# A decoder layer with 32 routed experts on one core: experts over 64 slots cut in two, scale and shift moved, the first branch hinted, the last norm reordered

## The chip, the core and the metric

The kernel runs on one core of a Trainium2 chip. The metric is the time of one execution in device microseconds (us), the median of several runs. The kernel before takes 1881.35 us (three runs, 1880.34 to 1883.35).

The core has five engines with one instruction stream each: TensorE (PE, matrix products), VectorE (DVE), ScalarE (ACT), GpSimd (POOL) and SyncE (SP). Transfers between the memory outside and the core's own memory go through DMA queues, which the engines feed. PE writes into PSUM, and DVE and ACT read from there.

## What is computed

One decoder layer for 512 tokens of width 1024. Two token mixers (a gated MLP and a dilated attention) give a residual sum, which a LayerNorm closes. Then come a second norm with scale and shift, a router that takes 4 of 32 experts for each token, the experts, and a last norm. Cut to the part that the change concerns:

```
h   = norm(t) * scale + shift                    # (512, 1024); t is the first LayerNorm's output
top_v, top_e = top_k(h @ w_router + b_router, 4)
top_w = softmax(top_v)
for each expert e, for its tokens:
    g = min(h @ w_gate[e] + b_gate[e], 7)
    u = clip(h @ w_up[e] + b_up[e], -7, 7)
    y[tok] += top_w * (((u + 1) * g * sigmoid(1.702 * g)) @ w_down[e] + b_down[e])
out = layer_norm(t * alpha + gate2 * y) * g2 + b2
```

Every expert has three matrices of 1024 x 1024 in f32, 12 MiB together. The reference's inputs are fixed, and so are its counts. Of the 2048 pairs of token and slot, experts 0 to 31 get: 8, 167, 35, 2, 43, 32, 124, 1, 71, 27, 74, 123, 44, 69, 14, 75, 12, 29, 58, 9, 45, 371, 58, 116, 34, 85, 169, 4, 26, 91, 6, 26. The kernel learns them only while it runs.

## The kernel before

**Front part** (to about 640 us). The token mixers run in f32 products made of three passes. For each of four blocks of 128 rows, `norms` makes both norms, and `route` the router's logits, the choice, and one-hot tables (tA, tC at L868, tV), from which PE sums up a slot table: for each expert, which token stands in which of its slots. `route` also scales and shifts h on POOL (L822, L823, two passes over 128 x 1024) and writes it to memory as h2d. From the table come the words `gidx` (rows to gather for each block of 128 slots, `gidx2` for half rows), `wslot` (weights of the slots) and `levw` (three bits for each expert: 0 for at most 64 slots, then one step for each further 64). The same table is waited for by the first gather.

**Expert stage** (from 641 us). The experts run in order, 0 to 31. The weights stream in as 384 units of 1 MiB, 12 for each expert (four of gate, four of up, four of down), into 17 buffers (`NLAND`). `free(u)` on SP starts the load of unit u + 17 once unit u has been used, so the stream runs 17 units ahead of PE at most. Each expert's rows are gathered from h2d by POOL, transposed on PE and copied to xT by ACT (`tr_x`, two copies of 128 x 512), one expert ahead.

What an expert does is chosen by `tc.If(lev > 0)` (L1356), which is a branch on every engine:

- `narrow` (at most 64 slots): the 64 columns of xT use half of PE's columns, so the matmuls run in two column groups, h = 0 and 1, each of which takes its own half of the weight's columns (gate L1088, up L1123, down L1146; biases L1053).
- `wide` (over 64 slots): all 128 columns of xT in full-width matmuls (gate L1091, up L1126, down L1149; biases L1049), and then, for over 128 slots, `further` blocks of 128 slots (L1179) behind a branch of their own (L1191). A further block with at most 64 slots runs like a narrow expert. A wide expert gives its gate's four buffers free only behind `further(e, 0)`, and its up's four behind `further(e, 1)`.

In both, `up` makes the first half of its columns, then the second, and transposes the first half's activations (`tr_act`, L1057) between matmuls of the second; `down` transposes the rest behind its third k tile. `y_out` (L1157) multiplies by the slot's weight and gate2 and adds the rows to ysum in memory by a scatter. `tr_x` for the next expert stands between up and down (`next_rows`). For branches, `mark_branch_hint_location` on PE names the branch that comes next. It stands behind the first bias of `up` for a narrow expert, behind the first k tile of `down` for a wide one; the first branch (expert 0) has none. The order of PE, ACT, DVE and SP in this stage is the order of the text (`manual_schedule`, L1350).

**Last norm** (`Finish`). The rows without the last expert's part are loaded while expert 31 runs; `early` (between gate and up) makes statistics and scaling of row blocks 0 and 1 on DVE, ACT and POOL, `middle` (between up and down) fetches the last expert's rows and treats blocks 2 and 3 on DVE (L1275 statistics, L1283 and L1284 scaling), and `add` treats the last expert's own rows.

Of the kernel before, what the change touches and what calls it, by code (L numbers as in the profile page):

```python
# [35 lines left out]
NLAND = 17  # L36


def host_consts():

    cst = np.zeros((P, 4 * P + NE), np.float32)
# [4 lines left out]
    cst[:, 3 * P + NE:] = np.eye(P)[::-1]  # L46
# [23 lines left out]
def layer(tc, I, out, dump=None, n_exp=NE):  # L70
# [27 lines left out]
    gidx = cp.tile([P, P], I32, name="gidx")  # L98
    wslot = cp.tile([P, P], F32, name="wslot")

    gidx2 = cp.tile([P, P], I32, name="gidx2")
    wslot2 = cp.tile([P, P], F32, name="wslot2")
    levw = cp.tile([1, 4], I32, name="levw")
# [329 lines left out]
    SP.dma_start(flip, I["cst"][:, 3 * P + NE:])  # L433
# [271 lines left out]
    for i in range(2):  # L705
        SP.dma_start(col2[:, i], rowd[1 + i].rearrange("(k p) -> p k", p=P))
    wr = f.tile([P, KT, NE], F32, name="wr")
# [10 lines left out]
    row("sc2", rowd[1:2])  # L718
    row("sh2", rowd[2:3])
# [4 lines left out]
    SP.dma_start(pow8, I["cst"][:, 3 * P:3 * P + NE])  # L724
    iota_e = iota[:, :NE]
# [87 lines left out]
    def route(r):  # L813
# [8 lines left out]
        G.tensor_tensor(h, h, rows["sc2"], op=ALU.mult)  # L822
        G.tensor_tensor(h, h, rows["sh2"], op=ALU.add)  # L823
# [27 lines left out]
        PE.matmul(pcnt, oneb, ohb_, start=r == 0, stop=r == 3)  # L851
# [73 lines left out]
    g2s = gp.tile([P, 512], F32, name="g2s")  # L925
    for n in range(2):
        SP.dma_start(g2s[H * n:H * n + H], rowd[3, 512 * n:512 * n + 512].partition_broadcast(H))
# [19 lines left out]
    tf2 = f.tile([P, P], F32, name="pj", bufs=2)  # L947
    for n in range(2):
        V.tensor_scalar(tf2[H * n:H * n + H], tf[:H], 2.0, float(n), op0=ALU.mult, op1=ALU.add)
    V.tensor_copy(gidx2, tf2)  # L950

    lw = f.tile([1, 4], F32, name="lw")
# [6 lines left out]
    V.tensor_reduce(lw, lv[:, 0].rearrange("p (a b) -> p a b", b=8), op=ALU.add, axis=AX)  # L959
# [6 lines left out]
    for n in range(2):  # L966
        V.tensor_copy(wslot2[H * n:H * n + H], wslot[:H])
# [13 lines left out]
def moe(tc, nc, I, E, main, env):  # L981
    (xrow, land, splA, landB, h2d, ysum, gidx, wslot, gidx2, wslot2, balld, selb, levw, ident, ysv, g2, g2s, yrow, y_init,
     out, epsT, after, last_dve, last_act) = (env[n] for n in (
         "xrow land splA landB h2d ysum gidx wslot gidx2 wslot2 balld selb levw ident ysv g2 g2s yrow y_init out epsT "
# [6 lines left out]
    def lev_words(engs):  # L991
        return [nc.values_load(levw[0:1, i:i + 1], engines=engs, min_val=0, max_val=(1 << 24) - 1,
                               skip_runtime_bounds_check_because="a sum of eight three-bit fields")
                for i in range(4)]

    words = lev_words([ET.PE, ET.Activation, ET.DVE, ET.Pool, ET.SP])
# [34 lines left out]
    ball_s = ball.rearrange("p (m s h c) -> p m s h c", m=2, s=2, h=2)  # L1031
    xT = sb.tile([P, KT, P], F32, name="xT")
    aT = sb.tile([P, KT, P], F32, name="aT")
    ga = sb.tile([P, D], F32, name="ga")

# [4 lines left out]
    ysum2 = ysum.rearrange("t (n f) -> (t n) f", n=2)  # L1040
# [11 lines left out]
    def bias_s(o, e, m, h, sts):  # L1052
        return PE.matmul(o, selb[:, e:e + 1].to_broadcast([96, H]), ball_s[:, m, sts, h], start=True, stop=False)  # L1053
# [19 lines left out]
    def gate(e, x, o, g, small, free=None, label=None):  # L1073
        u0 = 12 * e
        if small:
            r = [o[0][H * h:H * h + H].rearrange("p (s c) -> p s c", s=2) for h in range(2)]
            for h in range(2):
                end = bias_s(r[h], e, 0, h, slice(0, 2))
        else:
            for st in range(2):  # L1080
                end = bias(o[st], e, 0, st)
        hint(label, end)
        for kt in range(KT):
            w = W(u0 + kt // 2)[:, kt % 2]
            if small:
                w = w.rearrange("p (s h c) -> p s h c", s=2, h=2)
                for h in range(2):
                    PE.matmul(r[h], x[:, kt, :H], w[:, :, h], start=False, stop=kt == KT - 1)  # L1088
            else:
                for st in range(2):  # L1090
                    PE.matmul(o[st], x[:, kt], w[:, 512 * st:512 * st + 512], start=False, stop=kt == KT - 1)  # L1091
            if free and kt % 2:
                free(u0 + kt // 2)
        n = 512 if small else D
        for st in range(n // 512):
            V.tensor_scalar(g[:, 512 * st:512 * st + 512], o[st], LIMIT, None, op0=ALU.min)  # L1096
        S.activation(g[:, :n], g[:, :n], AF.Gelu_apprx_sigmoid)  # L1097

    def act_half(o, g):
# [3 lines left out]
    def tr_act(st, g, dst, small):  # L1103

        n = 2 if small else 4
        transposes(g[:, n * P * st:n * P * st + n * P], n, ptm[st])
        S.copy(dst[:, n * st:n * st + n], ptm[st][:, :n])  # L1107

    def up(e, x, o, g, dst, small, free=None, label=None):
        u0 = 12 * e + 4  # L1110
        for st in range(2):
            if small:
                for h in range(2):
                    end = bias_s(o[st][H * h:H * h + H, :256], e, 1, h, st)
# [112 lines left out]
    def next_rows(e):  # L1227
# [4 lines left out]
        if fin:  # L1232
            fin.middle()
# [162 lines left out]
```

## Time and profile before

| | |
|---|---|
| median of three runs | 1881.35 us (1880.34 to 1883.35) |
| profiled execution, its own time | 1875.77 us |
| its span (first to last instruction) | 1874.0 us |
| PE busy | 1746.6 us, 93% |
| PE weight loads (beside PE) | 991.6 us, 53% |
| DVE, ACT, POOL busy | 547.0, 382.3, 201.7 us |
| moved by DMA | 515.40 MB, 275 GB/s in the mean |

A profile is one execution, recorded by the chip. Its times are microseconds from the span's start. "Busy" is an average over the whole span; what bounds a stretch has to be read from that stretch: which engine is full in it, and, where one isn't, what ended its idle time. In the rows below a timeline's line is one instruction or several of the same kind in a row: start, duration, engine, line of the kernel, operation, output <- inputs, partitions x elements, count, and in brackets the idle time ahead of it with what ended it. "issue" there means that the engine waited for nothing that the profile shows. An engine's name with a q is its instruction sequencer. The granted clock (PEclk) is given as a share of full speed.

### The profile page before, as it was taken

What the parts mean: (1) busy time and instruction counts of PE and PEld (TensorE: products, weight loads), DVE (VectorE), ACT (ScalarE), POOL (GpSimd) and SP (SyncE); (2) the same over time, 40 slices, a digit from 0 to 9 for tenths busy, and PEclk for the clock granted to TensorE, in tenths of its full rate; (3) what the DMA queues carried; (4) which work ended last, traced back from release to release, by engine and by line L of the source; (5) the groups of instructions that cost most, each with busy time, mean ns of one, the idle gap of its engine ahead of it and who ended that gap; (6) DMA issues with size and microseconds to landing.
All of it is one profiled execution on the core that took longest, in us unless ns stands there. A gap on an engine that the chain in (4) does not pass through costs nothing. (4 is left out here: it accounts for less than half of the span.)

```text
span 1874.0 us, 20331 instructions
## 1 busy us (share of the span) xinstructions
PE 1746.6 (93%) x7590; PEld 991.6 (53%) x7590; DVE 547.0 (29%) x901; ACT 382.3 (20%) x745; POOL 201.7 (11%) x152
## 2 busy tenths in 40 slices
PE   6999999999997699999999999998899999899985
PEld 5777778788775444434444444443344444344432
DVE  7546656463279411111111111111011110111115
ACT  3533426255544200100000000011010000000001
POOL 2100000005023300110010001010100000001002
PEclk9999999999999699999999999999999999999998
DMA  8526352423253996999999999999971599949993
GB/s 281 197 88 210 109 191 75 174 68 105 85 187 136 352 366 238 404 404 404 398 390 399 346 380 375 364 399 404 402 284 32 198 401 395 351 170 326 406 384 120
DMA packets 159146, 515.40 MB, mean 275 GB/s; under 512 B 18298, under 2 KB 22858, under 8 KB 158870
## 3 DMA queue, kind: packets, MB, share of 16 engines
q1 hardware_dynamic: 147030, 490.74, 68.3%
q0 software_dynamic: 11840, 21.34, 4.6%
q8 instruction: 128, 2.10, 0.5%
q14 instruction: 148, 1.21, 0.2%
HBM read 504.21 MB, written 23.02 MB: 281 GB/s over the span
## 5 line engine op out<-in xcount | busy, mean ns | idle before, releaser
L1097 ACT ACTIVATE ga<-ga 128x512 f32<-128x512 f32 (+1 forms) x36 | 28.7, 796 | 573.8 <-DVE ga L1096 396.4
L1149 PE MATMUL po<-land,aT 128*128 128x512 f32 x320 | 141.5, 595 | 1.1 <-DVEq L1191 1.1
L166 PE MATMUL mm<-b,splA 128*128 128x512 f32 x352 | 138.8, 394 | 0.0
L167 PE MATMUL mm<-b,splA 128*128 128x512 f32 x352 | 137.9, 392 | 0.0
L168 PE MATMUL mm<-b,splA 128*128 128x512 f32 x352 | 137.8, 392 | 0.0
L1123 PE MATMUL pu<-land,xT 128*64 128x256 f32 x1024 | 129.2, 395 | 8.4 <-DMA land<-in_w_up_dram 8.4
L1091 PE MATMUL pg<-land,xT 128*128 128x512 f32 x288 | 127.7, 599 | 5.1 <-issue 5.1
L1126 PE MATMUL pu<-land,xT 128*128 128x512 f32 x288 | 128.8, 592 | 0.0
L111 DVE TENSOR_TENSOR splA<-land,splA 128x1024 fp32r<-128x1024 f32 x70 | 88.0, 1259 | 130.4 <-ACT splA L110 130.0
L1096 DVE TENSOR_SCALAR ga<-pg 128x512 f32<-128x512 f32 x44 | 30.4, 692 | 317.2 <-PE pg L1091 159.3
L1100 DVE TENSOR_SCALAR pu<-pu 128x256 f32<-128x256 f32 (+1 forms) x64 | 34.1, 533 | 297.6 <-PE pu L1126 160.9
L1088 PE MATMUL pg<-land,xT 128*64 128x512 f32 x504 | 115.3, 608 | 2.6 <-DMA land<-in_w_gate_dram 2.6
L1146 PE MATMUL po<-land,aT 128*64 128x512 f32 x448 | 105.1, 607 | 7.6 <-ACT aT L1107 7.6
L110 ACT CAST splA<-land 128x1024 fp32r<-128x1024 f32 x72 | 75.4, 1051 | 178.1 <-PE mm L168 142.7
L1123 PEld LDWEIGHTS pu<-land,xT 128*64 128x64 f32 x1024 | 74.4, 142 | 53.1 <-DMA land<-in_w_up_dram 13.6
L1107 ACT COPY aT<-ptm 128x256 f32<-128x256 f32 (+1 forms) x64 | 28.9, 451 | 357.8 <-PE ptm L1057 357.8
L1149 PEld LDWEIGHTS po<-land,aT 128*128 128x128 f32 x320 | 59.4, 190 | 70.3 <-issue 67.9
L1091 PEld LDWEIGHTS pg<-land,xT 128*128 128x128 f32 x288 | 55.2, 192 | 72.9 <-issue 70.4
L1044 POOL DMA_INDIRECT xrow<-h2d,gidx x32 | 34.0, 1061 | 541.7 <-PE ptm L1057 530.2
L1126 PEld LDWEIGHTS pu<-land,xT 128*128 128x128 f32 x288 | 53.6, 190 | 66.0 <-issue 64.6
L166 PEld LDWEIGHTS mm<-b,splA 128*128 128x128 f32 x352 | 66.2, 188 | 17.0 <-ACT splA L110 2.6
L1088 PEld LDWEIGHTS pg<-land,xT 128*64 128x64 f32 x504 | 37.0, 140 | 71.2 <-issue 62.4
(379 smaller groups left out, 2514.1 us busy)
## 6 DMA issues: line engine op xcount, KB each, us to landing
land<-in_w_up_dram SPq DMA_DIRECT2D x100, 1024.0 KB, 15.2
land<-in_w_gate_dram SPq DMA_DIRECT2D x99, 1024.0 KB, 18.1
land<-in_w_down_dram SPq DMA_DIRECT2D x96, 1024.0 KB, 18.6
splA<-in_w_down_dram SPq DMA_DIRECT2D x32, 1024.0 KB, 16.4
land<-in_w_in_dram SPq DMA_DIRECT2D x30, 1024.0 KB, 5.2
splA<-in_w_gate_dram SPq DMA_DIRECT2D x29, 1024.0 KB, 20.1
splA<-in_w_up_dram SPq DMA_DIRECT2D x28, 1024.0 KB, 15.8
land<-in_w_ada_dram SPq DMA_DIRECT2D x24, 1024.0 KB, 6.2
```

The source lines that it names most:

```text
L110: hi = S.copy(w[:, 0], src)
L111: return hi, eng.tensor_tensor(w[:, 1], src, w[:, 0].bitcast(F32), op=ALU.subtract)
L166: PE.matmul(o, l[0], r[0], start=start, stop=False)
L167: PE.matmul(o, l[0], r[1], start=False, stop=False)
L168: return PE.matmul(o, l[1], r[0], start=False, stop=stop)
L1088: PE.matmul(r[h], x[:, kt, :H], w[:, :, h], start=False, stop=kt == KT - 1)
L1091: PE.matmul(o[st], x[:, kt], w[:, 512 * st:512 * st + 512], start=False, stop=kt == KT - 1)
L1100: V.tensor_scalar(o, o, LIMIT, -LIMIT, op0=ALU.min, op1=ALU.max)
L1123: PE.matmul(o[st][H * h:H * h + H, :256], x[:, kt, :H], w[:, 256 * h:256 * h + 256], start=False, stop=kt == KT - 1)
L1126: PE.matmul(o[st], x[:, kt], w, start=False, stop=kt == KT - 1)
L1146: end = PE.matmul(o[0][H * n:H * n + H], a[:, 2 * st + b, H * h:H * h + H], wn, start=ft == 0, stop=ft == KT - 1)
L1149: end = PE.matmul(o[n], a[:, ft], wn, start=ft == 0, stop=ft == KT - 1)
```

## The change

1. **Scale and shift.** POOL's two passes over h go away: h2d holds the plain norm. `tr_x` scales and shifts while it copies: four pieces of 128 x 128 on ACT and four on DVE, with the scale and shift as columns (`colh`).
2. **First branch.** A hint for `expert0` behind the last matmul that counts (`pcnt`, in `route` of block 3).
3. **Buffers.** 18 instead of 17.
4. **Wide experts.** Their first 64 slots are worked like a narrow expert (two column groups). Slots 64 to 127 are a second part ("b"), worked ahead of the first one: in two column groups, too, if the expert has over 96 slots, and otherwise in four groups of 32 columns (n = 4). Which, is chosen by a new branch (`either`) at gate, up and down. Up of the first part is now one pass over k for all columns (`both_halves`); down transposes both halves ahead of its first matmul (`both=True`). There are two `y_out`, with tables of their own for the second part, and a new word with one bit for each expert (over 96). The hint for the next expert isn't set in a wide expert. Further blocks stay as they are.
5. **Last norm.** `early` scales block 0 alone; `middle` scales block 1 and makes the statistics of block 2 on ACT; the new `late` makes those of block 3 on ACT and scales both. The rows' fetch is moved into `next_rows`. `add` has a form for the second part.

```diff
-NLAND = 17
+NLAND = 18
...
-        G.tensor_tensor(h, h, rows["sc2"], op=ALU.mult)
-        G.tensor_tensor(h, h, rows["sh2"], op=ALU.add)
         SP.dma_start(h2v[:, r], h)
...
-        PE.matmul(pcnt, oneb, ohb_, start=r == 0, stop=r == 3)
+        cnt = PE.matmul(pcnt, oneb, ohb_, start=r == 0, stop=r == 3)
+        if r == 3:
+            with after(cnt):
+                tc.mark_branch_hint_location("expert0", engines=[ET.PE])
...
     def tr_x(src, dst):
         for a in range(2):
             transposes(src[:, 512 * a:512 * a + 512], 4, ptm[a])
-            S.copy(dst[:, 4 * a:4 * a + 4], ptm[a])
+            for i in range(4):
+                kt = 4 * a + i
+                if a:
+                    V.tensor_scalar(dst[:, kt], ptm[a][:, i], colh[:, 0, kt:kt + 1], colh[:, 1, kt:kt + 1],
+                                    op0=ALU.mult, op1=ALU.add)
+                else:
+                    S.activation(dst[:, kt], ptm[a][:, i], AF.Identity, scale=colh[:, 0, kt:kt + 1],
+                                 bias=colh[:, 1, kt:kt + 1])
...
+    def both_halves(e, u0, m, x, o, n, free, label=None, t0=0):
+        r = [group(o, h, n).rearrange("p (s c) -> p s c", s=2) for h in range(n)]
+        for h in range(n):
+            end = bias_s(r[h], e, m, h, slice(0, 2), n)
+        hint(label, end)
+        for kt in range(KT):
+            w = W(u0 + kt // 2)[:, kt % 2].rearrange("p (s h c) -> p s h c", s=2, h=n)
+            for h in range(n):
+                PE.matmul(r[h], x[:, kt, t0:t0 + P // n], w[:, :, h], start=False, stop=kt == KT - 1)
...
-    def wide(e, lev, levP):
+    def wide(e, lev, levP, more96):
+        def either(f):
+            with tc.If(more96 > 0, preferred_fallthrough_block=True) as c:
+                f(2)
+            with c.Else():
+                f(4)
+        def gate_b(n):
+            both_halves(e, 12 * e, 0, xT, pg[1], n, None, t0=H)
+            V.tensor_scalar(gb[:, :D // n], pg[1][:, :D // n], LIMIT, None, op0=ALU.min)
+            S.activation(gb[:, :D // n], gb[:, :D // n], AF.Gelu_apprx_sigmoid)
+        def up_b(n):
+            both_halves(e, 12 * e + 4, 1, xT, pu[1], n, None, t0=H)
+            act(pu[1][:, :D // n], gb[:, :D // n])
+        def down_b(n):
+            down(e, aTb, po[1:], gb, n, both=True)
+            y_out(e, 0, po[1:], yb, n, True)
         rows_ahead(e, levP)
-        gate(e, xT, pg, ga, False, label=f"further{e}_0")
+        either(gate_b)
+        gate(e, xT, pg, ga, 2, label=f"further{e}_0")
         further(e, 0, lev)
         for q in range(4):
             free(12 * e + q)
         if fin:
             fin.early()
-        up(e, xT, pu, ga, aT, False, label=f"further{e}_1")
+        either(up_b)
+        both_halves(e, 12 * e + 4, 1, xT, pu[0], 2, None, f"further{e}_1")
+        act(pu[0], ga[:, :512])
...
         further(e, 1, lev)
         for q in range(4, 8):
             free(12 * e + q)
         next_rows(e)
-        down(e, aT, po, ga, False, free=free, label=f"expert{e + 1}" if e + 1 < E else None)
-        y_out(e, 0, po, yrow, False)
+        either(down_b)
+        down(e, aTa, po, ga, 2, both=True, free=free)
+        y_out(e, 0, po, yrow, 2)
...
         def early(self):
             for r in range(2):
                 self.spread(r, self.x[r])
-            for r in range(2):
-                self.scale_act(r, self.x[r])
-                self.store(r)
+            self.scale_act(0, self.x[0])
+            self.store(0)
 
         def middle(self):
-            self.fetch(0)
+            self.scale(1, self.x[1])
+            self.store(1)
+            self.spread_act(2, self.x[2])
+
+        def late(self):
+            self.spread_act(3, self.x[3])
             for r in (2, 3):
-                self.spread(r, self.x[r])
                 self.scale(r, self.x[r])
                 self.store(r)
```

## Rows read from the trace of the kernel before

**Rows 1.** Busy time by stretch: window, us; five engines (count); PEclk, DMA share, GB/s.

```profile
641.00:750.00 109.00, 105.81 (x496) 49.41 (x498) 13.53 (x23) 9.99 (x17) 11.12 (x8) 0.98 0.85 313
750.00:1030.00 280.00, 270.38 (x1155) 119.89 (x1151) 34.41 (x57) 23.96 (x44) 23.83 (x18) 0.99 1.02 400
1030.00:1340.00 310.00, 291.70 (x1314) 129.44 (x1313) 37.50 (x63) 25.59 (x47) 23.84 (x18) 0.98 0.98 381
1340.00:1490.00 150.00, 144.32 (x408) 64.63 (x406) 18.61 (x27) 11.12 (x18) 10.26 (x8) 1.00 0.51 189
```

**Rows 2.** PE's timeline in expert 20, narrow.

```profile
1332.28 1.98 PE L1123 MATMUL pu<-splA,xT 128*64 128x256 f32 x8 [1.48 <-DMA splA<-in_w_up_dram]
```

**Rows 3.** PE's timeline in expert 6, wide, to the next expert's first bias.

```profile
838.39 13.90 PE L1091 MATMUL pg<-land,xT 128*128 128x512 f32 x32
853.13 0.38 PE L1049 MATMUL pu<-ball,selb 96*128 96x512 bf16 x1 [0.84 <-DVEq L1191]
...
865.16 2.74 PE L1126 MATMUL pu<-splA,xT 128*128 128x512 f32 x6
...
869.48 3.70 PE L1149 MATMUL po<-splA,aT 128*128 128x512 f32 x8 [0.21 <-DVEq L1191]
...
883.85 0.41 PE L1053 MATMUL pg<-ball,selb 96*64 96x512 bf16 x2
```

**Rows 4.** PE's timeline in expert 2, narrow: half of gate, then up's bias.

```profile
741.02 3.60 PE L1088 MATMUL pg<-splA,xT 128*64 128x512 f32 x16
744.45 0.28 PE L1053 MATMUL pu<-ball,selb 96*64 96x256 bf16 x2
```

**Rows 5.** Timelines of DVE, POOL and PE ahead of the expert stage.

```profile
573.48 0.69 DVE L868 TENSOR_TENSOR tC<-cst_s,bk 128x512 fp32r<-128x512 f32 x1
583.80 1.28 DVE L806 SCALAR_TENSOR_TENSOR lt<-lt,l1rs,row_ln_b 128x1024 f32<-128x1024 f32 x1
599.94 2.86 DVE L805 SCALAR_TENSOR_TENSOR lt<-lt,l1nm,row_ln_g 128x1024 f32<-128x1024 f32 x1
614.67 2.82 DVE L868 TENSOR_TENSOR tC<-cst_s,bk 128x512 fp32r<-128x512 f32 x1
...
614.28 2.67 POOL L823 TENSOR_TENSOR h<-h,row_sh 128x1024 f32<-128x1024 f32 x1
...
571.23 0.18 PE L850 MATMUL pl<-ohbf,trib 128*128 128x32 bf16 x1 [2.20 <-DVE ohbf L845]
```

**Rows 6.** Branches on PE's sequencer: count, then ns least/median/most, first and last start.

```profile
L1356 PEldq COMPARE_BRANCH  x44: 81/340/7769, 633.5 to 1823.2; - x44
...
L1356 PEldq COMPARE_BRANCH  x2: 318/2949/5580, 876.1 to 876.7; - x2
...
L1356 PEldq COMPARE_BRANCH  x1: 6192/6192/6192, 1721.8 to 1721.8; - x1
...
L1191 PEldq COMPARE_BRANCH  x30: 77/344/3472, 673.4 to 1775.6; - x30
```

**Rows 7.** PE's timeline, first records behind four long branches (experts 0, 26, 28, 30).

```profile
641.42 0.67 PE L1053 MATMUL pg<-ball,selb 96*64 96x512 bf16 x2 [6.82 <-issue]
...
1630.56 3.47 PE L1091 MATMUL pg<-land,xT 128*128 128x512 f32 x5 [3.41 <-issue]
...
1728.00 0.41 PE L1053 MATMUL pg<-ball,selb 96*64 96x512 bf16 x2 [2.59 <-issue]
...
1801.71 0.41 PE L1053 MATMUL pg<-ball,selb 96*64 96x512 bf16 x2 [4.33 <-issue]
```

**Rows 8.** ACT's timeline ahead of the expert stage.

```profile
617.59 2.45 ACT L898 ACTIVATE tW<-tC,twh 128x128 fp32r<-128x128 f32 x8 [5.96 <-DVE tC L868]
```

**Rows 9.** PE's timeline in the front part: sixteen small matmuls, each with its weight load.

```profile
557.54 0.63 PE L910 MATMUL pl<-wr,col 128*1 128x32 f32 x16
```

**Rows 10.** Timelines of PE and DVE at the end.

```profile
1853.71 3.58 PE L1146 MATMUL po<-land,aT 128*64 128x512 f32 x8 [7.65 <-ACT aT L1107]
...
1865.20 1.28 DVE L1284 SCALAR_TENSOR_TENSOR yrow<-yrow,frs,splA 64x1024 f32<-64x1024 f32 x1
```

More of the change, by code (lines that the diff above doesn't have):

```diff
@@ L989, in moe, with lev_words @@
     ps = ms.enter_context(tc.tile_pool(name="pM", bufs=1, space=PSUM, reuse_waits="tile"))
-    def lev_words(engs):
+    gidx = gidxs[1]
+    def lev_words(engs, r=range(4)):
         return [nc.values_load(levw[0:1, i:i + 1], engines=engs, min_val=0, max_val=(1 << 24) - 1,
-                               skip_runtime_bounds_check_because="a sum of eight three-bit fields")
-                for i in range(4)]
-    words = lev_words([ET.PE, ET.Activation, ET.DVE, ET.Pool, ET.SP])
+                               skip_runtime_bounds_check_because="a sum of eight three-bit or sixteen one-bit fields")
+                for i in r]
+    every = [ET.PE, ET.Activation, ET.DVE, ET.Pool, ET.SP]
+    words = lev_words(every)
+    words96 = lev_words(every, (4, 5))
     wordsP = lev_words([ET.Pool])
@@ L1071, in hint, with group, gate @@
                 tc.mark_branch_hint_location(label, engines=[ET.PE])
-    def gate(e, x, o, g, small, free=None, label=None):
+    def group(o, h, n, c=None):
+        return o[P // n * h:P // n * h + P // n, :c or D // n]
+    def both_halves(e, u0, m, x, o, n, free, label=None, t0=0):
[7 more added lines that the diff above has]
+                PE.matmul(r[h], x[:, kt, t0:t0 + P // n], w[:, :, h], start=False, stop=kt == KT - 1)
+            if free and kt % 2:
+                free(u0 + kt // 2)
+    def gate(e, x, o, g, n, free=None, label=None):
         u0 = 12 * e
[L1075 to L1078, printed above, removed]
+        if n > 1:
+            both_halves(e, u0, 0, x, o[0], n, free, label)
         else:
@@ L1081, in gate @@
                 end = bias(o[st], e, 0, st)
[L1082 to L1089, printed above, removed]
+            hint(label, end)
+            for kt in range(KT):
+                w = W(u0 + kt // 2)[:, kt % 2]
                 for st in range(2):
@@ L1091, in gate @@
                     PE.matmul(o[st], x[:, kt], w[:, 512 * st:512 * st + 512], start=False, stop=kt == KT - 1)
[L1092 to L1099, printed above, removed]
+                if free and kt % 2:
+                    free(u0 + kt // 2)
@@ L1100, in act_half, with act @@
+        c = D // n
+        for st in range(-(-c // 512)):
+            V.tensor_scalar(g[:, 512 * st:min(c, 512 * st + 512)], o[st][:, :min(c, 512)], LIMIT, None, op0=ALU.min)
+        S.activation(g[:, :c], g[:, :c], AF.Gelu_apprx_sigmoid)
+    def act(o, g):
         V.tensor_scalar(o, o, LIMIT, -LIMIT, op0=ALU.min, op1=ALU.max)
         V.scalar_tensor_tensor(g, o, 1.0, g, op0=ALU.add, op1=ALU.mult)
[L1103 to L1107, printed above, removed]
@@ L1111, in up @@
         for st in range(2):
-            if small:
-                for h in range(2):
-                    end = bias_s(o[st][H * h:H * h + H, :256], e, 1, h, st)
+            if n > 1:
+                for h in range(n):
+                    end = bias_s(group(o[st], h, n, c), e, 1, h, st, n)
             else:
@@ L1232, in next_rows @@
         if fin:
-            fin.middle()
+            fin.fetch(0)
     def rows_ahead(e, levP, j=1):
@@ L1261, in __init__ @@
             self.last = W(NU - 14)
+            self.back, self.more = xrow[:H], gaj[1][:H]
             self.x = [self.rows[i // 2][:, i % 2] for i in range(4)]
@@ L1264, in __init__ @@
             self.mv = [sb.tile([P, 2], F32, name=f"fmv{i}") for i in range(5)]
+            self.sm = [sb.tile([P, 4], F32, name=f"fsm{i}") for i in range(2)]
             self.rs, self.nb = (sb.tile([P, 5], F32, name=n) for n in ("frs", "fnb"))
```

223 lines of the change are left out of this document (134 added, 89 removed).

## The prediction

> **What bounds the kernel now.** I read the stretches of the expert stage first, with the DMA share beside TensorE (PE) [rows 1], then PE's timeline through single experts [rows 2 to 4]. Two bounds take turns. From about 750 to 1340 us the DMA share is 1.02 and 0.98: the weight stream runs full, and PE waits for a weight buffer ahead of its matmuls, as in the 1.48 us in expert 20 [rows 2]. From expert 21 (371 slots) to the end PE is the bound: the share falls to 0.51 while that expert is worked [rows 1], the stream then only refills buffers, and PE's idle stretches are named "issue", not DMA. So an edit of PE's work is worth its full size after 1340 us, and before it only what the stream still idles. Ahead of 750 us the buffers are full and PE is late, so an earlier start there moves everything behind it.
>
> A narrow expert spends 6.86 us on each of its three matrices: 16 records, half a matrix, last 3.43 us from start to start [rows 4]. A wide one without further blocks takes 45.9 us, from 838.39 to 883.85 and its own bias, 0.44 us [rows 3]. The reference's routing gives twelve experts over 64 slots: 8, 10, 13, 15, 25, 29 hold 69 to 91, and 1, 6, 11, 21, 23, 26 over 96.
>
> **The change, part by part.** The profiled execution took 1875.77 us, the median is 1881.35. I work out a difference on the former and subtract it from the median.
>
> (a) Scale and shift leave GpSimd (POOL): minus 9. While POOL runs its two passes over h, VectorE's (DVE) instructions stretch: a norm's pass takes 2.86 us where it takes 1.28 with POOL idle, tC 2.82 against 0.69 [rows 5]. There are two of each kind (norm passes, one-hot tables) in the last two row blocks; they lose 1.6 + 1.5 + 1.6 + 2.1 = 6.8 us just ahead of the slot table for which the first gather waits. I take 5.5, since with DVE faster the router's logits become late. Three earlier norm passes lose 5.5 more, and PE then waits for DVE twice, once 2.20 us [rows 5]; I take 3.5. Against it, some fourteen small DVE instructions are added, 0.2 us each; those behind the table fall into the wait for the first gather. Bounds: minus 4 (one of the two places) to minus 12 (all).
>
> (b) The hint ahead of the first branch: minus 5.5. PE's first branch is the longest of its line, 7.77 us (the median is 0.34) [rows 6], and leaves PE idle for 6.82 us [rows 7]. What is late then is xT: ScalarE (ACT) and DVE each do four pieces side by side, 0.31 us each as the eight of line 898 in 2.45 us [rows 8], instead of two ACT copies in a row; it is complete near 635.9, and the gate starts there instead of at 641.42. Bounds: minus 3 (a hinted branch of 3 us) to minus 6.
>
> (c) Up to expert 21: minus 6. PE time saved there only becomes a longer wait for weights; what can be had is the stream's own idle time. The share is 0.98 against 1.02 over 310 us [rows 1], so some 12 us. It idles where a wide expert holds four buffers until its whole gate or up is done; experts 13 and 15 now hold them for less time, the 18th buffer covers one transfer more, but expert 11 stays as long as it was. I take half; 0 to minus 12.
>
> (d) A wide expert on PE. The first 64 slots cost three narrow matrices, 20.6 us. The second part is split in four column groups of 32 if it has at most 32 slots. Nothing in the trace runs four groups. Two overlap fully: a pair of their records takes the 0.43 us of one full-width record [rows 3, 4]. Four records of half the columns would then take 0.215 us, a matrix 3.43 us. Issue doesn't forbid it: 16 matmuls with their weight loads start within 0.63 us [rows 9], so four need less than 0.16. The other end is that four overlap no more than two do: 6.86 us. I take 3.43, as the pair is the nearest row.
> What is added: PE stands through a round trip that the old order hid. After up, eight transposes take some 1.4 us; the second part's transposes must wait until ACT has read one PSUM tile (four pieces) and DVE the other (behind two instructions of up's own, 0.69 us each by tC's size), to about 2.7 us, and then for a copy: the first down matmul comes 3.4 us after up, where now it is 1.5 us (up's last records end near 867.9, down starts at 869.48) [rows 3]. Then transposes and two copies stand alone ahead of the main down, 1.1 us. At the ends of the three new Ifs an engine makes up semaphore counts; the join behind gate, 0.84 us [rows 3], stays, and I take 0.4 us for each new one. Sum for at most 96 slots: 3 x (6.86 + 3.43) + 0.9 (biases) + 0.84 + 3.4 + 1.1 + 3 x 0.4 = 38.3, minus 7.6. For over 96 slots: 10.3 more and longer copies, some 48.9, plus 3. After 1340 us there are two of the first (25, 29) and three of the second (21, 23, 26): minus 15.2 and plus 9, with 0.8 for the longer copies in further blocks. Bounds: minus 10 to plus 2.7 each for the first, 0 to plus 5 for the second.
>
> (e) Branches at a wide expert's end: plus 7. The sequencer runs ahead of the array. Behind full-width matmuls it spent 0.32 and 5.58 us in two branches at 876 [rows 6], and PE's next record still came at 883.85 with no idle time [rows 3]. Behind two column groups a branch of 6.19 us [rows 6] left PE idle for 2.59 us [rows 7], so 3.6 us was covered. The change ends every wide expert with two-group matmuls, and drops the hint there. So 0.32 + 5.6 - 3.4 = 2.5 to 2.7 us are bared from 21 to 22, 23 to 24 and 26 to 27: plus 8. From 25 into 26, where 3.41 us is bared now, plus 2; the present 2.59 and 4.33 us at 28 and 30 are due anew at new code places, minus 3 [rows 7]. The new branches inside a wide expert jump over blocks shorter than the further ones of line 1191, whose median is 0.34 us [rows 6]; that lies under the queue. Bounds: minus 4 to plus 25.
> [...]
>
> (f) The last norm: minus 7. PE waits 7.65 us for aT in the last down [rows 10], because that copy stands on ACT behind a root that waits for DVE's scaling, itself stretched by POOL. In the new order the copy comes after one block's statistics on ACT, some 3.4 us begun when up's first copy is done, and down ends near 1850. Then DVE is late: three row blocks of scaling (two passes of 1.28 us each, one of them stretched) from 1843.2 to about 1852.1, then 7.3 us for the last rows, to 1859.4, where the last pass now ends at 1866.5 [rows 10]. Bounds: minus 4 to minus 8.
>
> **The sum.** Minus 9, 5.5 and 6; then minus 15.2, plus 9.8, plus 7, minus 7: minus 25.9. 1881.35 - 26 = 1855 us. A measurement of this kernel tells about 0.2% (3.8 us) from no change.
>
> **Rivals.**
> 1. Four groups are no faster than two. Then a small second part costs 6.86 us a matrix; experts 25 and 29 lose 10.3 us each, and (c) goes: 1855 + 20.6 + 6 = 1882, no change. For: no row shows four groups. Against: the pair's full overlap. [...]
> 2. Instruction fetch takes over (slower). A wide expert's code grows by six blocks. If branches inside it miss as the longest further branch does, 3.47 us [rows 6], and the lead behind four groups covers little, the three Ifs bare 3 us each, and the end 4.7 (7.77 + 0.32 - 3.4) instead of 2.7. For the five wide experts after 1340 us that is 5 x 9 + 4 x 2 = 53, so 1908, and up to 1930 with what the stream before doesn't absorb. It decides from 26 / 5 = 5.2 us per wide expert on. For: misses of over 5.5 us at the outer branch. Against: the inner median.
> 3. More is had: the stream's whole idle time, no join costs, cheap ends by luck of the code's place: minus 6, 6 and 5, so 1838.
> 4. The stream, not PE, holds back the first experts, and (a) and (b) are swallowed: 1869. Against: a share of 0.85 there [rows 1].
>
> **How the numbers follow.** Forecast 0.62, rival 1 0.10, rival 2 0.12, rival 3 0.13, rival 4 0.03. The forecast's own bounds reach from about 1840 to 1872. The range runs from rival 3's middle, 1836, to just short of rival 1's, 1880, and leaves out rival 2 and some of 1 and 3. Faster by over 0.2%: the forecast, rivals 3 and 4, a little of 1: 0.80. Same: most of 1: 0.07. Slower: rival 2 and a rest of 1: 0.13.
>
> **What would show it.** (a) tC and the norm passes of the last row blocks at 0.7 and 1.3 us, the first gather some 9 us earlier. (b) No 6.8 us gap ahead of the first gate. (c) Expert 21's first matmul near 1328, the DMA share to there at 1.0. (d) Expert 25 in some 38 us, 23 in 49, four-group records 0.05 us apart. (e) 2 to 3 us of "issue" behind 21, 23 and 26. (f) No wait of 7 us for aT. The forecast is wrong if expert 25 isn't some 7 us shorter, if "issue" or joins inside wide experts add up to over 5 us each, or if expert 21 starts no earlier than 1340.

## The result, and the profile after

The changed kernel takes 1908.58 us (four runs, 1907.96 to 1914.81) against 1880.84 us (1879.54 to 1883.35) of the kernel before in the same job: a ratio of 1.0153, 95% interval 1.013 to 1.0177. The forecast was 1855 us, faster. The profiled execution took 1914.81 us, some 6 us over its median; its span is 1913.1 us, and its mean granted clock 0.956 where it was 0.974. One execution of the kernel before (2050.40 us, granted clock 0.84) and the profiled one of two_groups below (2094.75 us, 0.838) fell into a slower state: both are left out, so two_groups has no trace to compare.

First the expert stage by stretches, with the columns of [rows 1]:

```profile
641.00:750.00 109.00, 98.95 (x532) 40.48 (x530) 16.45 (x33) 11.78 (x26) 11.83 (x9) 0.95 0.83 306
750.00:1030.00 280.00, 246.82 (x1576) 104.53 (x1576) 44.19 (x93) 27.44 (x69) 25.35 (x19) 0.96 1.00 386
1030.00:1340.00 310.00, 276.63 (x1798) 114.48 (x1791) 46.61 (x97) 29.56 (x74) 30.09 (x22) 0.94 0.93 350
1340.00:1490.00 150.00, 137.24 (x504) 57.63 (x501) 22.01 (x39) 11.50 (x23) 7.95 (x6) 0.98 0.62 240
```

PE is busy for less of each stretch than in [rows 1] (246.82 for 270.38 us, 276.63 for 291.70): it has less work, and it stands more often, as the table below shows. The DMA share fell too, to 0.93 from 1030 to 1340 us, and the granted clock is 0.94 to 0.96 in the first three stretches, where it was 0.98 and 0.99.

What PE waited for in the expert stage (waiting line and releaser: us in total, times, longest):

```profile
PE pg L1079 <- issue: 52.6, 13, 9.3
PE ptm L1083 <- issue: 11.5, 8, 1.8
PE ptm L1083 <- PEq L1234: 8.3, 10, 2.3
PE pu L1079 <- PEq L1234: 6.6, 3, 2.4
PE pu L1079 <- DVEq L1234: 6.3, 7, 0.9
PE ptm L1083 <- ACT xT L1095: 6.2, 5, 1.2
PE pu L1119 <- issue: 6.0, 3, 4.7
```

The first line is the gate's bias, the first record of an expert: 46.4 of the 52.6 us stand at the ends of eleven wide experts. Before the change the same wait was 13.7 us, half of it ahead of expert 0, and only one of the wide experts' ends had such a wait (4.33 us). The `further` branch is L1234 now (L1191 before), the expert's branch L1453 (L1356), the new choice L1248.

From expert 0's first record to the last record of the last down, the traces add up like this. Idle is time without a matmul; of the busy time at a granted clock of 0.5, half is put down as lost; the rest is work at the full clock.

| us | before | after | hints_early | old_wide |
|---|---|---|---|---|
| expert 0 starts | 641.4 | 630.3 | 631.4 | 632.2 |
| work at the full clock | 1140.5 | 1087.6 | 1090.8 | 1139.3 |
| PE idle | 61.5 | 129.7 | 108.2 | 55.4 |
| lost at half clock | 15.6 | 46.0 | 22.5 | 11.0 |
| from the last down to the end | 15.0 | 19.5 | 19.5 | 16.9 |
| span | 1874.0 | 1913.1 | 1872.4 | 1854.8 |

So the change removed 53 us of PE work and 11 us ahead of it, and added 68 us of idle time, 30 us at half clock and 4.5 us at the end (the two last columns are experiments, below). Expert 8 (71 slots, four groups) shows how, on PE's timeline:

```profile
919.90 1.47 PE L1119 MATMUL pg<-land,xT 128*32 128x256 f32 x24
923.02 1.50 PE L1119 MATMUL pg<-land,xT 128*32 128x256 f32 x24 [1.65 <-issue]
...
930.71 1.88 PE L1119 MATMUL pg<-splA,xT 128*64 128x512 f32 x8
934.95 0.29 PE L1079 MATMUL pu<-ball,selb 96*32 96x256 bf16 x4 [2.36 <-PEq L1234]
935.07 0.60 PE L1119 MATMUL pu<-splA,xT 128*32 128x256 f32 x5
940.32 4.24 PE L1119 MATMUL pu<-splA,xT 128*32 128x256 f32 x42 [4.65 <-issue]
...
955.45 0.33 PE L1083 MATMUL ptm<-cst_s,ga 128*128 128x128 f32 x1 [1.23 <-ACT xT L1095]
...
956.30 3.66 PE L1191 MATMUL po<-land,aT 128*32 128x256 f32 x64
...
960.80 7.09 PE L1191 MATMUL po<-land,aT 128*64 128x512 f32 x32 [0.24 <-ACT aT L1150]
972.04 0.64 PE L1079 MATMUL pg<-ball,selb 96*64 96x512 bf16 x2 [4.16 <-issue]
```

The four-group matrix takes 3.66 us and the two-group one 7.09: the work is as forecast. Between them stand 1.65, 2.36, 4.65 and 4.16 us of nothing. The branches on PE's sequencer that belong to the second and the last (columns as in [rows 6]):

```profile
L1234 PEldq COMPARE_BRANCH  x1: 6170/6170/6170, 928.3 to 928.3; - x1
...
L1453 PEldq COMPARE_BRANCH  x2: 931/4144/7357, 963.4 to 964.6; - x2
```

The sequencer reaches the `further` branch at 928.25, some 4.3 us ahead of the end of gate's last records (932.59), and stands there for 6.17 us. Before, that branch took 0.34 us in the median [rows 6]. I call a branch missed where it takes over 1 us.

What goes with such a branch stands in the trace too. Two of the DMA queues are of the kind "instruction", and one of them, q8, moves 16 KiB at a time. From 935.6 to 940.4 us, around the wait of 4.65 us (columns: packets, MB, share of 16 engines):

```profile
q8 instruction: 1, 0.02, 1.5%
```

That packet landed at 938.83 us, 1.49 us before PE went on. In the changed kernel each of the 34 branches of over 2.5 us on PE's sequencer has such a landing within it (mostly 1.3 to 1.5 us before its end), and none of the 96 under 0.5 us has one; before the change it is 18 of 18 and none of 66. So a fetch of instructions goes with each of the long branches, and with this wait without a branch. From expert 0's first record on there are 154 of these packets, where there were 105.

The half clock mostly follows idle time. A window behind expert 6's end (idle for 3.37 us), columns as above:

```profile
893.40:899.20 5.80, 5.79 (x16) 1.85 (x18) 0.00 (x0) 0.00 (x0) 1.55 (x1) 0.50 1.02 405
```

Sixteen records take 5.79 us there; at the full clock of 883.85 us [rows 3] as many took some 3.2. From expert 0's first record to the end of the last down the changed kernel has 21 stretches at 0.5, the lower of the two levels in the trace, and the kernel before seven.

### The profile page after: what moved, and what is told of

Read it like the earlier page. It is cut to its first block, busy times and chain, and to the rows that moved or that the text cites. A ratio compares the mean times of both kernels' runs of the same rounds, so it can differ in the third digit from the quotient of the medians.

```text
span 1913.1 us, 24621 instructions
## 1 busy us (share of the span) xinstructions
PE 1723.5 (90%) x9378; PEld 944.5 (49%) x9378; DVE 577.6 (30%) x1058; ACT 404.9 (21%) x864; POOL 194.6 (10%) x154
## 5 line engine op out<-in xcount | busy, mean ns | idle before, releaser
L1119 PE MATMUL pg<-land,xT 128*64 128x512 f32 (+1 forms) x1320 | 265.4, 587 | 7.0 <-DMA land<-in_w_gate_dram 4.0
L1191 PE MATMUL po<-land,aT 128*64 128x512 f32 (+1 forms) x1240 | 233.5, 563 | 3.9 <-ACT aT L1150 3.7
L1119 PEld LDWEIGHTS pg<-land,xT 128*64 128x64 f32 (+1 forms) x1320 | 88.0, 142 | 170.7 <-issue 152.0
L1191 PEld LDWEIGHTS po<-land,aT 128*64 128x64 f32 (+1 forms) x1240 | 73.2, 135 | 127.9 <-issue 108.3
L1143 DVE TENSOR_SCALAR pu<-pu 128x256 f32<-128x256 f32 (+1 forms) x64 | 32.5, 508 | 279.7 <-PE pu L1119 154.5
L1139 DVE TENSOR_SCALAR ga<-pg 128x512 f32<-128x512 f32 x32 | 22.1, 692 | 282.9 <-PE pu L1079 203.3
L1119 PE MATMUL pu<-land,xT 128*64 128x512 f32 (+1 forms) x672 | 106.3, 507 | 1.3 <-issue 1.3
L1095 ACT ACTIVATE xT<-ptm,colh 128x128 f32<-128x128 f32 x144 | 54.2, 456 | 200.1 <-PE ptm L1083 200.1
L1218 DVE SCALAR_TENSOR_TENSOR yrow<-po,wslot,g 128x512 f32<-128x512 f32 x31 | 23.3, 751 | 204.7 <-PE po L1191 204.7
L1191 PE MATMUL po<-splA,aT 128*64 128x512 f32 (+1 forms) x360 | 75.5, 590 | 0.0
L165 PEld LDWEIGHTS mm<-b,splA 128*128 128x128 f32 x352 | 66.2, 188 | 16.9 <-ACT splA L109 2.6
L1219 POOL DMA_INDIRECT ysum<-yrow,gidx x31 | 48.9, 1576 | 240.9 <-DVE yrow L1218 181.6
## 6 DMA issues: line engine op xcount, KB each, us to landing
land<-in_w_up_dram SPq DMA_DIRECT2D x98, 1024.0 KB, 10.5
splA<-in_w_gate_dram SPq DMA_DIRECT2D x21, 1024.0 KB, 19.7
```

Of the source, the lines that this page charges most:

```text
L165: PE.matmul(o, l[0], r[0], start=start, stop=False)
L1095: S.activation(dst[:, kt], ptm[a][:, i], AF.Identity, scale=colh[:, 0, kt:kt + 1], bias=colh[:, 1, kt:kt + 1])
L1119: PE.matmul(r[h], x[:, kt, t0:t0 + P // n], w[:, :, h], start=False, stop=kt == KT - 1)
L1143: V.tensor_scalar(o, o, LIMIT, -LIMIT, op0=ALU.min, op1=ALU.max)
L1191: end = PE.matmul(group(o[0], q, n), l, w[:, D // n * q:D // n * q + D // n], start=ft == 0, stop=ft == KT - 1)
L1219: G.indirect_dma_start(out=ysums[n], out_offset=bass.IndirectOffsetOnAxis(ap=rows, axis=0), in_=y[:, :w], in_offset=None, bounds_check=n * ...
```

## The experiments

The first theory (A): the branches. A hint that stands ahead of 7 us of two-group matmuls instead of 14 us of full-width ones comes too late for its branch, and the queue in front of it covers less. The rival (B): the cut itself, with its new Ifs, joins and round trips. Leads (from the hint to its branch on PE's sequencer) are mostly 9.0 to 10.1 us ahead of the hinted `further` branches before the change and 4.2 to 7.0 us after it.

### The cut undone, all else kept: old_wide

```diff
-        either(gate_b)
-        gate(e, xT, pg, ga, 2, label=f"further{e}_0")
+        gate(e, xT, pg, ga, 1, label=f"further{e}_0")
...
-        either(up_b)
-        both_halves(e, 12 * e + 4, 1, xT, pu[0], 2, None, f"further{e}_1")
-        act(pu[0], ga[:, :512])
+        up(e, xT, pu, ga, aT, 1, label=f"further{e}_1")
...
-        either(down_b)
-        down(e, aTa, po, ga, 2, both=True, free=free)
+        down(e, aT, po, ga, 1, free=free, label=f"expert{e + 1}" if e + 1 < E else None)
```

> The changed kernel with the wide experts of before (full-width matmuls, the old hints); scale and shift in the copies, the first hint, 18 buffers and the last norm's order stay changed. Theories A and B alike: expert 0 starts some 11 us earlier, the last norm gives some 4 us net, the stream some more: 1858 to 1868 us, so that the wide experts alone cost 40 to 50 us in the changed kernel. A third theory (C: the loss comes from the moved scale and shift, or from the stream with 18 buffers): 1890 us or more.

Measured: 1855.13 us, ratio 0.9881 (0.9853 to 0.9909), below both kernels. So the cut costs 51 to 53 us, and all else gains 23 to 26, a few us more than was expected. The price shows where theory A looks: behind expert 0 the gate's bias waits for "issue" for 0.9 us in total instead of 52.6. One more thing shows at the end, on DVE's timeline:

```profile
1820.85 1.29 DVE L1350 BATCH_NORM_STATS2 fst<-land 128x6 f32<-128x512 f32 x2 [6.59 <-DMA land<-ysum]
```

Expert 31 begins at 1804.5, and `early` waits 6.59 us for the rows that it treats; PE then waits 8.1 us for DVE. An expert 31 that starts sooner loses part of it there.

### The hints moved ahead: hints_early, next_hint_only

The hints go into the second part, and away from their old places:

```diff
-            both_halves(e, 12 * e, 0, xT, pg[1], n, None, t0=H)
+            both_halves(e, 12 * e, 0, xT, pg[1], n, None, f"further{e}_0", t0=H)
...
-            both_halves(e, 12 * e + 4, 1, xT, pu[1], n, None, t0=H)
+            both_halves(e, 12 * e + 4, 1, xT, pu[1], n, None, f"further{e}_1", t0=H)
...
-            down(e, aTb, po[1:], gb, n, both=True)
+            down(e, aTb, po[1:], gb, n, both=True, label=f"expert{e + 1}" if e + 1 < E else None)
```

> The changed kernel with the hints of a wide expert moved ahead: for the further branches behind the first bias of the second part (gate and up), for the next expert behind the first k tile of the second part's down. The leads become some 8 us (four groups) and 11 us (two). Theory A: the further branches fall back to some 0.35 us, most of the idle time named issue inside the wide experts goes, and most of the half-clock spells behind it: 25 to 45 us faster than the changed kernel, 1865 to 1885 us. Theory B: within 5 us of the changed kernel, 1903 to 1913 us. A third possibility: the branch between hint and target (over 96 slots or not) takes the hint's place, and the leads do nothing.

Measured: 1875.68 us, ratio to before 0.9991 (0.9976 to 1.0007), 31 to 33 us less than the changed kernel with the same PE work. So theory A has the larger part of the loss. Its waits:

```profile
PE pg L1079 <- issue: 37.2, 13, 7.3
PE ptm L1083 <- issue: 9.9, 7, 2.2
PE pu L1079 <- DVEq L1234: 8.1, 9, 0.9
```

The `further` branches add up to 33.8 us instead of 75.9, not to the 14.6 of before: with leads of mostly 8 to 13 us some still miss. The wide experts' ends keep 34.2 us of idle time. That is why the cut gains nothing even so: against old_wide, hints_early has 48.5 us less work, 52.8 more idle time and 11.5 more lost at half clock. next_hint_only is the last of the three edits alone.

> The changed kernel with one hint more: for the next expert, behind the first k tile of the second part's down in a wide expert; the further branches' hints stay where the change put them. It splits the 33 us that hints_early gave back. At a wide expert's end the missed jump should fall from some 7.4 to some 5.5 us, behind a queue of 2.6 us: 1.9 us less idle time at each of twelve ends, and fewer half-clock spells behind them: 12 to 24 us faster than the changed kernel, 1885 to 1897 us. If the further branches alone made the loss: 1903 us or more.

Measured: 1906.74 us, ratio to before 1.0145 (1.0114 to 1.0175), 2 us less than the changed kernel: outside the 12 to 24 us that were expected. The jumps at a wide expert's end did fall to 4.9 to 6.3 us, and the gate's bias waits 41.9 us for "issue", not 52.6. In its trace expert 31 starts 11.6 us sooner, and then takes 6 us longer, half of which is waiting as in old_wide. The profiled execution of the changed kernel is also 6 us over its median. By the medians some 30 of hints_early's 31 to 33 us are left for the hints of the `further` branches; by the start of expert 31 in the traces it is 29 of 40. These hints alone were not moved.

### What a missed branch costs behind full-width matmuls: late_hints, no_further_hints, no_next_hint

In the kernel before, first with the hints for the `further` branches moved behind the third k tile of gate and the fifth of up's first half:

> The kernel before, and in its wide experts the hints for the two further branches stand some 5 us later: behind the third k tile of gate, and behind the fifth k tile of up's first half, instead of behind the first bias. Nothing else moves. Theory A (the lead from hint to branch decides): the further branches, 0.35 us with a lead of 9 to 10 us in the kernel before, take 2 to 6 us with a lead of 4 to 5 us, as in the changed kernel; some 1 to 2 us of each is bared ahead of up and behind it, and the clock falls behind some of them: 20 to 45 us slower, 1900 to 1925 us. Theory B (what costs is the cut of the wide experts itself: new Ifs, joins, waits for transposes): no change, 1877 to 1885 us.

Measured: 1876.3 us, ratio 0.9993 (0.9978 to 1.0008). It says little: most leads in its trace are still 6.4 to 9.0 us, and the branches short. The one lead of 3.7 us (expert 11) has a branch of 5.88 us. So the hints were taken away altogether:

```diff
-        gate(e, xT, pg, ga, False, label=f"further{e}_0")
+        gate(e, xT, pg, ga, False)
...
-        up(e, xT, pu, ga, aT, False, label=f"further{e}_1")
+        up(e, xT, pu, ga, aT, False)
```

> The kernel before without any hint for the further branches. It measures how much of a missed branch the queue behind full-width matmuls hides. The branches should take 6 to 7.5 us where the hinted ones take 0.35. If the queue holds some 6 us of full-width work, 0 to 1.5 us of each is bared, ten of them after 1340 us: 1878 to 1895 us. If a queue covered only 2.6 us, as behind two-group matmuls, 4 us each: 1915 us or more.

Measured: 1873.11 us, ratio 0.9969 (0.9953 to 0.9985), no loss at all, and below what was expected. Thirteen of the thirty branches take 3.3 to 6.2 us; all thirty make 77.6 us, as much as in the changed kernel (75.9). Expert 6, the branch and then PE's timeline:

```profile
L1191 PEldq COMPARE_BRANCH  x1: 5942/5942/5942, 847.9 to 847.9; - x1
...
841.64 13.90 PE L1091 MATMUL pg<-land,xT 128*128 128x512 f32 x32
856.38 0.38 PE L1049 MATMUL pu<-ball,selb 96*128 96x512 bf16 x1 [0.84 <-DVEq L1191]
```

The same 0.84 us as with the hint [rows 3]: at 847.88 PE has 7.6 us of gate still to run. A miss of 6 us is free there, and bares some 2 us (2.36 in expert 8) behind the 4.3 us that two-group matmuls leave.

> The kernel before without the hint for the next expert in a wide expert's down. In the changed kernel, which has none, the branch behind a wide expert takes 7.1 to 8.0 us where it takes 5.4 to 6.0 us before. Theory A: the same here, so 1 to 2 us more for each, of which the full-width down (a queue of some 7 us) covers nearly all; up to 2 us for each of the three narrow experts behind a wide one after 1340 us: 0 to 8 us slower, 1881 to 1889 us. Theory B: no change.

Measured: 1875.38 us, ratio 0.9985 (0.9973 to 0.9997). Without the hint the jump takes 7.0 to 7.5 us eight times, as in the changed kernel, and full-width down hides that too.

### The cut without its branch: two_groups, two_groups_hints, four_groups_hints

```diff
-            with tc.If(more96 > 0, preferred_fallthrough_block=True) as c:
-                f(2)
-            with c.Else():
-                f(4)
+            f(2)
```

> The changed kernel without its new branch: the second part of a wide expert runs in two column groups always, so four groups and the choice between them are gone; the hints stay where the change put them. Each of the six experts with at most 96 slots gets 3 x 3.4 = 10 us more of PE work. Theory A (hints that come too late for their branch, and a queue behind two-group matmuls that covers only 2.6 us): the further branches still have some 4.4 us from hint to branch and take 2 to 6 us; 1895 to 1925 us. Theory B (the new branch and its joins are what costs): 1875 to 1890 us.

Measured: 1925.73 us, ratio 1.0237 (1.0202 to 1.0272). Without the new branch the loss stays, where theory B forecast 1875 to 1890 us. But six experts have 10 us more of PE work each, so the branch isn't priced by this alone.

> The same with the hints moved ahead (further branches: first bias of the second part; next expert: first k tile of the second part's down). No other branch stands between hint and target. Theory A: leads of 11 us, the further branches at some 0.35 us, 15 to 35 us faster than two_groups, 1880 to 1900 us, a wide expert of at most 128 slots in 50 to 52 us plus a bared end of some 2.7 us. If the leads do nothing: as two_groups.

Measured: 1909.67 us, ratio 1.0143 (1.0095 to 1.019), 16 us less by the hints alone, though over the 1880 to 1900 us expected. The `further` branches of this kernel, then those of four_groups_hints:

```profile
L1234 PEldq COMPARE_BRANCH  x30: 72/280/3853, 666.2 to 1816.0; - x30
...
L1234 PEldq COMPARE_BRANCH  x30: 72/352/2020, 662.1 to 1734.2; - x30
```

Their sum is 14.4 us here, that of before, with leads of 9.9 us and more, and 19.3 us in four_groups_hints, with leads down to 6.5. That hints_early keeps more (33.8) could come from the choice of the groups between hint and target, as its third possibility had it. Its trace speaks against that: in the experts with at most 96 slots PE's sequencer runs no branch between the two, and their twelve `further` branches make 18.6 us of the 33.8; in experts 6, 11 and 23, where one stands between, six make 10.5. Nor does the lead settle a single branch: in the changed kernel six jumps with leads of 4.2 to 6.8 us take 5.8 to 6.5 us, as long as without any hint (up to 6.2 us in no_further_hints). What else decides is open. Expert 23 takes 50.0 us, 1.8 of it the wait at its end; the forecast was 48.9. But two two-group passes (2 x 7.09 us) are no shorter than one full-width pass (13.90 us [rows 3]), so all that is added to a wide expert is loss.

> As two_groups_hints, but the second part runs in four groups always, so slots 96 to 127 are left out of experts 1, 6, 11, 21, 23 and 26. It prices the cut without the new branch. Every wide expert then has 10.3 us for each matrix; theory A: 37 to 39 us for experts 25 and 29, a bared end of 2.7 us, no idle time at the further branches: 1835 to 1858 us. Theory B with the joins alone as the cause: experts 25 and 29 still at 41 us or more.

Measured: 1841.41 us, ratio 0.9797 (0.9762 to 0.9832). It leaves out slots 96 to 127 of experts 1, 6, 11, 21, 23 and 26, so it prices the cut and is no kernel to use. Expert 25 takes 39.16 us. Twelve experts with 3 x 3.43 us less PE work each are 123 us; 68 us of them arrive (against two_groups_hints).

### A cut without branches inside: small_cut, small_cut_first

Built on old_wide. Experts of 65 to 96 slots get a block of their own: gate and up cut in two and four groups, down at full width, no branch within. One If more chooses the block:

```diff
             with tc.If(lev > 0, preferred_fallthrough_block=True, label=f"expert{e}") as more:
-                wide(e, lev, levP, (words96[e // 16] >> (e % 16)) & 1)
+                with tc.If(((words96[e // 16] >> (e % 16)) & 1) > 0, preferred_fallthrough_block=True) as c96:
+                    wide(e, lev, levP)
+                with c96.Else():
+                    small(e)
```

> Built on old_wide (1855 us): experts with over 96 slots run as before; those with 65 to 96 slots run a block of their own without any branch in it: gate and up are cut (two groups for the first 64 slots, four groups for the next 32), down runs at full width, so that the queue ahead of the next branch holds as much work as before. One more branch chooses between the two blocks, ahead of gate; the block for over 96 slots stands first. Theory A (the cut pays where no branch stands behind two- or four-group matmuls): experts 25 and 29 take 38 to 41 us instead of 45.8, less 3 us for a missed branch ahead of each; the stream takes most of what 8, 10, 13 and 15 gain: 1842 to 1853 us. If the cut never pays: 1855 us or more.

Measured: 1869.95 us, ratio 0.9951 (0.9929 to 0.9972): 13 to 15 us over old_wide where a gain was expected. Expert 29 is all that was hoped for, from 1758.45 to 1796.18 us, 37.7 for 45.9. Ahead of and behind the wide experts it is lost again. Two branch lines behind expert 6 and PE's next record:

```profile
L1484 PEldq COMPARE_BRANCH  x2: 6145/6184/6222, 872.0 to 907.5; - x2
L1483 PEldq COMPARE_BRANCH  x2: 88/2850/5612, 878.5 to 907.1; - x2
...
884.15 0.64 PE L1080 MATMUL pg<-ball,selb 96*64 96x512 bf16 x2 [4.30 <-issue]
```

Two jumps in a row miss, 6.2 us and 5.6, more than full-width down covers. There are sixteen waits of this kind, 54.8 us together (5.7 of them ahead of expert 0); behind expert 0, old_wide has 0.9.

> The same with the block for at most 96 slots first. The missed branch then falls to the experts with over 96 slots (21, 23, 26 after 1340 us) instead of 25 and 29: within 5 us of small_cut; the sign follows from where the jumps miss: ahead of 21, 23 and 26 (each behind a narrow expert's two-group down or expert 25) some 3 us bared, and none ahead of 25 and 29.

Measured: 1873.94 us, ratio 0.998 (0.9967 to 0.9993). The order of the blocks changes who pays, and little of the sum.

### One buffer less: old_wide_17

> old_wide with 17 buffers instead of 18. It prices the 18th buffer by itself. If it gives what the forecast let it give up to expert 21 (one more transfer covered): 0 to 6 us slower than old_wide, 1855 to 1861 us, with the difference up to expert 21.

Measured: 1861.45 us, ratio 0.9922 (0.9894 to 0.9951), against old_wide's 0.9881 (0.9853 to 0.9909). The intervals overlap, so the 18th buffer's gain isn't clear of noise; in the traces expert 21 starts 3.6 us later, all of it from expert 5 on, where PE waits longer for weights.

## Why the prediction was wrong, point by point

In the traces the forecast is missed by 65 us (54 by the medians), and 50 of them lie ahead of expert 21's first record: 20.5 us less were forecast to there, and it is 29.7 more. Behind it 15 us are missing.

**(a) Scale and shift: right.** The first gather starts 7.8 us sooner (POOL's issue of the two first gathers, here of before), for 9 forecast, with the tables and norm passes of the last blocks at the durations that were named:

```profile
L1044 POOL DMA_INDIRECT xrow<-h2d,gidx x2: 1058/1074/1090, 625.4 to 634.9; - x2
```

And after, with one norm pass and one table (DVE's timeline):

```profile
L1070 POOL DMA_INDIRECT xrow<-h2d,gidx x2: 1037/1063/1089, 617.6 to 626.9; - x2
...
597.36 1.27 DVE L805 SCALAR_TENSOR_TENSOR lt<-lt,l1nm,row_ln_g 128x1024 f32<-128x1024 f32 x1
...
607.42 0.69 DVE L869 TENSOR_TENSOR tC<-cst_s,bk 128x512 fp32r<-128x512 f32 x1
```

**(b) The first hint: the lower bound.** The branch takes 4.2 us instead of 7.77, and PE waits 3.70 us where it waited 6.82 [rows 7], minus 3.1 for the 5.5 forecast. Together expert 0 starts 11.1 us sooner, for 14.5.

**(c) Up to expert 21: wrong in sign for this kernel.** In old_wide expert 21 starts 10.5 us sooner than before with a start that is 9.2 sooner, so what the stream still idles gave 1.3 us and not 6. In the changed kernel expert 21 starts 29.7 us late. I took the stream as a bound that swallows what PE gains, and counted no loss there; but a PE that stands holds its buffers, and the stream stands with it. SP, which starts the loads, waits from 750 to 1340 us for PE's `further` branches as follows, in the changed kernel, then in hints_early:

```profile
SPq L1047 <- PEq L1234: 108.8, 11, 15.6
...
SPq L1047 <- PEq L1234: 64.4, 11, 12.4
```

Before the change it was 63.7 us. The DMA share from 640 to 1340 us is 0.94 in the changed kernel, and 0.98 in hints_early and before. Some 40 of the 58 us between the traces of the changed kernel and old_wide were lost by expert 21's start, in a stretch which the sum priced with the one gain; hints_early, which gives its buffers back at the same places of the text, starts expert 21 32.5 us sooner than the changed kernel.

**(d) PE's work: right.** Rival 1 is out: a four-group matrix takes 3.66 us and less, half of a two-group one. Experts 25 and 29 fell from 45.8 to 41.2 us and from 50.3 to 44.5, ends and idle time included, for 38.3 forecast. Expert 23 rose by 7.9 us, for 3: 4.0 us of its 53.8 are the wait at its end. Without misses inside and without that wait it is 48.2 (two_groups_hints), so the round trip and the joins were sized well, and the rest is idle time and clock.

**(e) Branches: the step that failed.** "That lies under the queue" took the new Ifs alone into account, and these are short indeed: 25.0 us for 54, four of them misses. The old `further` branches were left at their 0.34 us. But the hint for them stood behind the bias of a gate of 14 us, and now stands behind the bias of one of 7: the lead fell to 4.2 to 7.0 us, and thirty branches rose from 14.6 to 75.9 us, with 19.7 instead of 2.8 at the Ifs within. At the same time the work queued ahead of them shrank from some 7.6 to some 4.3 us. At the experts' ends the jump rose from 5.6 to some 7.4 us without its hint, and mostly 3.3 to 4.7 us were bared (from 2.2 to 9.3), for 2.5 to 2.7; and I counted that behind 21, 23, 25 and 26 alone, while eleven ends lost 46.4 us. PE's idle time is 68 us more in all. What a long branch does to the time hangs here on the queue ahead of it: in no_further_hints, behind some 7.6 us of it, thirty branches of 77.6 us in sum lost nothing. That there is a fetch in the long ones is seen in the landings on q8, one within each of the 34.

A term was missing altogether: the clock. Idle times of some 2 to 9 us were mostly followed by stretches at half clock (five of the 21 stretches follow waits of under 2 us alone), which cost 30 us more than before. That they follow the idle time is seen in the traces; nothing here took the one away without the other.

**(f) The last norm: right in kind.** PE's wait of 7.65 us is gone; DVE is last, as forecast:

```profile
1884.35 0.41 PE L1083 MATMUL ptm<-cst_s,ga 128*128 128x128 f32 x2 [1.78 <-DVE ga L1144]
...
1886.04 2.74 PE L1191 MATMUL po<-land,aT 128*64 128x512 f32 x12
...
1902.82 1.28 DVE L1363 SCALAR_TENSOR_TENSOR splA<-splA,frs,land 64x1024 f32<-64x1024 f32 x1
```

From expert 31's first record to the end of the span it is 43.6 us, from 47.3: 3.7 less, and not 7. Overlooked was the wait for the rows that `early` treats: 1.90 us here, 6.59 in old_wide.

**The rivals.** Rival 2 gave 1908 us, which is what was measured, and its kind was right: instruction fetch, decided per wide expert. Its sum was not, so the number is luck. It put 9 us on each of the five wide experts after 1340 us, at the new Ifs; the trace has the misses at the `further` branches and at the ends, most of the loss ahead of 1340 us, and nearly a third of it as clock. The chance of 0.12 was too small because its "against" (the inner median of 0.34 us) was read from branches whose hints stood 10 us ahead, and the edit moved the hint's lead.

## What to carry to other kernels

A branch is priced from the new code, not by its duration in the old (thirty `further` branches took 14.6 us in sum before the change and 75.9 after it), and three numbers mattered here: how long ahead its hint stands (9.0 to 10.1 us, then 4.2 to 7.0), how much work is queued on the engine in front of it (some 7.6 us, then 4.3), and how many jumps follow each other (two in small_cut, 6.2 and 5.6 us). Two-group matmuls, 7.09 us a matrix for 13.90, shrank the first two; the hints moved ahead gave back 31 to 33 us. The stretch bound by its weight stream took little of what PE gained (1.3 us in old_wide), but it took stalls of PE that held buffers (some 40 us).

## What the runs showed of the hardware that was not expected

- Four column groups of 32 overlap fully in f32: 64 records of 128x256 take 3.66 us, half of the 7.09 us of 32 two-group records of 128x512 for a matrix of the same size.
- Behind full-width f32 matmuls thirty branches of 77.6 us in sum, thirteen of them of 3.3 to 6.2 us, cost nothing (no_further_hints: 1873.11 us, ratio 0.9969); some 7.6 us of work was queued there, and some 4.3 us behind two-group ones.
- The idle times that the misses left were mostly followed by a granted clock of 0.5: 21 stretches for seven.
- A fetch of instructions can be seen in the DMA queues: each of the 34 branches of over 2.5 us has a landing of 16 KiB on q8 within it, none of the 96 under 0.5 us has.
- PE also stood for 4.65 us in the middle of four-group matmuls, with no branch record behind 934.9 us; such a landing came 1.49 us before it went on. Why a fetch was due there is left open.
